# A transformer block with a split-precision MLP: two Strassen products after the chunk loop in place of the plain ones inside it

## The chip, the cores and the metric

One core of a Trainium2 chip runs the whole kernel. The metric is the device time of one launch in microseconds (us), the median of several runs. The engines are named as in the profile: PE is the matmul engine and PEld its weight loads, DVE the vector engine, ACT the scalar engine, POOL the GpSimd engine; SP issues all DMAs of this kernel.

## The reference

2048 tokens `x` of 1024 channels (`D`) pass one block. First an attention branch and a pooling branch, merged by gates, projected, added to `ALPHA * x` and layer-normalised. Then the part that the change touches, with `DFF` = 4096 hidden columns:

```python
def _mlp_sublayer(z, shift, scale, gate, w1, w2, g, b):
    u = _modulate(z, shift, scale)
    h = jnp.square(jax.nn.relu(u @ w1)) @ w2
    return _layernorm(ALPHA * z + gate * h, g, b)
```

Everything is fp32. The result before is a [2048, 1024] array.

## The kernel before, in words

PE multiplies fp32 numbers as products of two parts: `split` (L52) writes a high part (a rounding cast, by ACT) and a low part (the rest, by DVE, or by POOL where `lo_eng` says so), and each product is three matmuls, high by high, high by low and low by high (`mm3`, L59, and `chan_mm`, L680). Nearly all of the MLP's matmuls stream 512 columns against 128 by 128 stationary elements, and each has a weight load of its own.

Phase 1 (to about 865 us) makes `u`, q, k, v and the attention output and spills `u` and the output to DRAM (`u_scr`, `a_scr`). Phase 2 is a loop over two chunks `c` of 1024 tokens (L717). A chunk loads its `u` (`load_u`, L556: DMA into `raw`, then `split` into slots), does the pooling branch (`p_group`, `p_finish`, `pool_gate`), the attention gates, the branch products and the merge (`mg`), and the output projection (`out_mm`, L870). Per block `b` of 128 tokens follow `ln_affine` (the first layer norm, L891) and `ln1_u`, which normalises once more into `xn`; `u2_half` (L912) turns four blocks at a time on PE, modulates them on ACT and splits them. `accs[b]` holds the block's residual in SBUF through the MLP.

The MLP is the end of the chunk's body. For each group `fg` of 256 hidden columns, `mlp_in` (L945) multiplies `u2` with `w_mlp_in`, takes ReLU on ACT, squares on DVE and splits into `ht`; `mlp_out` (L959) multiplies `ht` with `w_mlp_out`, already scaled by the gate `gb[1]` on POOL, and DVE adds the product to `accs[b]`. After the last group `ln2` normalises and stores. The group after is always computed before the output product of this one, so that PE has work while ACT, DVE and POOL finish `ht`.

The slots are two sets, `a` (right side) and `b` (left side), 8 or 9 tiles for each of two tags, which change their parts between the chunks: `xs` takes `u`, `av`, then `accs`, `xn` and `ht`; `ys` takes the pooling tiles, `mg` and `u2`. Weights come through two `raw` tiles and two pairs `wh`, `wl`. A scheduler orders each engine's instructions by simulated time where the program doesn't fix it; a tile's slot comes free when the tile's last reader is done. All DMAs stand in one queue on SP, so a DMA that waits holds those behind it.

Numbers that the steps need: a chunk's MLP is 16 groups, each with 2 columns of 128, 2 halves of 512 tokens, 8 k tiles and 3 matmuls for the first product, and 8 blocks, 2 halves, 2 k tiles and 3 matmuls for the second: 16 * (96 + 96) = 3072 matmuls of 512 columns, 6144 for both chunks.

## Time and profile before

| what | value |
|---|---|
| runs | 3176.19 us median of 3 (3172.74 to 3176.82) |
| profiled execution, first to last instruction | 3174.3 us |
| PE busy | 3096.2 us, 98% of the span |
| DVE, ACT, POOL busy | 56%, 36%, 36% |
| chain that ended last | PE 87%, DVE 7% |
| DMA | 207.04 MB, mean 65 GB/s |

The profiled execution's own time is known as its span alone; the median is 1.9 us above it. The share of PE is a share of time in which any matmul is under way. Matmuls overlap, so one of 512 columns is shown as about 395 ns long though the next one starts earlier; the pace is read from how many start in a stretch.

### The profile page before, as it was taken

Reading aid. Unit: us, or ns where it says so; the run is one execution under the profiler, and the core shown is the slowest. Engines: PE = TensorE matmul, PEld = TensorE weight load, DVE = VectorE, ACT = ScalarE, POOL = GpSimd, SP = SyncE. Lnnn points to the kernel's source line nnn. Section 1 sums busy time; section 2 is a strip of 40 time slices with the busy share of each in tenths; the row PEclk is TensorE's granted clock in tenths of the full one; section 3 lists DMA queues with packets and bytes.
Section 4 is the critical chain, followed back from the end, with each engine's and each line's share of the span. In section 5 each row is a group of like instructions: output and inputs, shape, how many; then the busy total and the mean of one; then the engine's idle time right before and its main releaser. Section 6 shows DMA issues by size and latency. Waiting matters only on the chain.

```text
span 3174.3 us, 41663 instructions
## 1 busy us (share of the span) xinstructions
PE 3096.2 (98%) x16104; PEld 2616.7 (82%) x16104; DVE 1780.8 (56%) x3136; ACT 1128.2 (36%) x1985; POOL 1151.8 (36%) x1419
## 2 busy tenths in 40 slices
PE   8899999998999999899999999999999999999998
PEld 5799899997988889788888888788898788888886
DVE  5678788887774446644444455821448444444446
ACT  4577777777621222521112112311214311121111
POOL 2877777776420052422122221410234321222123
PEclk9999999999999999999999999999999999999999
DMA  7111111113154430211111112411321111111111
GB/s 244 35 30 41 35 31 41 35 31 105 28 160 128 146 107 28 67 41 53 53 41 54 40 53 66 142 52 40 107 93 54 40 53 44 50 53 41 53 40 53
DMA packets 157846, 207.04 MB, mean 65 GB/s; under 512 B 7248, under 2 KB 132304, under 8 KB 157648
## 3 DMA queue, kind: packets, MB, share of 16 engines
q1 hardware_dynamic: 157648, 204.38, 20.5%
q8 instruction: 127, 2.08, 0.3%
q14 instruction: 71, 0.58, 0.1%
HBM read 179.19 MB, written 25.17 MB: 64 GB/s over the span
## 4 chain that ended last, share of the span: by engine, by line
PE 87%; DVE 7%; DMA 2%; issue 2%; POOL 1%; ACT 1%; SPq 0%; DVEq 0%; POOLq 0%; ACTq 0%
PE ps_y L62 7%; PE ps_y L63 7%; PE ps_y L61 7%; PE ps_h L677 7%; PE ps_h L680 7%; PE ps_h L678 7%; PE ps_o L497 4%; PE ps_pt L480 4%; PE ps_s L444 3%; PE ps_ga L677 2%; PE ps_ga L680 2%; PE ps_ga L678 2%; PE ps_ab L677 2%; PE ps_ab L678 2%; PE ps_ab L680 2%; PE ps_s L445 2%
## 5 line engine op out<-in xcount | busy, mean ns | idle before, releaser
L57 POOL TENSOR_TENSOR ht<-r,ht 128x512 fp32r<-128x512 f32 x128 | 172.0, 1346 | 1009.0 <-ACT ht L54 946.3
L974 DVE TENSOR_TENSOR acc<-ps_y,acc 128x512 f32<-128x512 f32 x464 | 314.7, 689 | 366.6 <-PE ps_y L63 366.5
L54 ACT CAST wh<-raw 128x2048 fp32r<-128x2048 f32 (+1 forms) x102 | 189.1, 1857 | 828.9 <-PE ps_y L63 471.6
L678 PE MATMUL ps_h<-u,wh 128*128 128x512 f32 x1024 | 406.2, 397 | 10.3 <-DVE u L57 10.3
L62 PE MATMUL ps_y<-wl,ht 128*128 128x512 f32 x1024 | 405.0, 396 | 1.7 <-DVE wl L57 1.7
L680 PE MATMUL ps_h<-u,wl 128*128 128x512 f32 x1024 | 404.7, 396 | 0.0
L63 PE MATMUL ps_y<-wh,ht 128*128 128x512 f32 x1024 | 403.2, 394 | 0.0
L677 PE MATMUL ps_h<-u,wh 128*128 128x512 f32 x1024 | 401.3, 398 | 0.0
L61 PE MATMUL ps_y<-wh,ht 128*128 128x512 f32 x1024 | 400.6, 393 | 0.0
L57 DVE TENSOR_TENSOR wl<-raw,wh 128x2048 fp32r<-128x2048 f32 (+1 forms) x100 | 228.1, 2282 | 202.8 <-ACT wh L54 202.8
L951 DVE TENSOR_TENSOR r<-r 128x512 f32<-128x512 f32 x128 | 142.7, 1119 | 300.6 <-ACT r L950 300.6
L57 DVE TENSOR_TENSOR pl<-ps_pt,ph 128x512 fp32r<-128x512 f32 x312 | 212.6, 686 | 70.4 <-ACT ph L54 68.4
L678 PEld LDWEIGHTS ps_h<-u,wh 128*128 128x128 f32 x1024 | 193.2, 189 | 57.0 <-DVE u L57 12.1
L459 POOL TENSOR_SCALAR s<-s,sm 128x640 f32<-128x640 f32 (+1 forms) x256 | 202.3, 798 | 99.1 <-DVE sm L458 53.7
L456 ACT ACTIVATE s<-s,sm 128x641 f32<-128x641 f32 (+1 forms) x256 | 210.2, 822 | 66.6 <-DVE sm L450 66.1
L62 PEld LDWEIGHTS ps_y<-wl,ht 128*128 128x128 f32 x1024 | 192.1, 188 | 47.6 <-DVE wl L57 2.3
L61 PEld LDWEIGHTS ps_y<-wh,ht 128*128 128x128 f32 x1024 | 192.3, 188 | 46.9 <-ACT r L950 0.3
L680 PEld LDWEIGHTS ps_h<-u,wl 128*128 128x128 f32 x1024 | 193.5, 189 | 45.4
L677 PEld LDWEIGHTS ps_h<-u,wh 128*128 128x128 f32 x1024 | 193.2, 189 | 45.1
L450 DVE CUSTOM_DVE_ANT_0 s<-ps_s,mask,nsink 128x640 f32<-128x640 f32 (+1 forms) x256 | 211.4, 863 | 31.2 <-PE ps_s L445 30.6
L63 PEld LDWEIGHTS ps_y<-wh,ht 128*128 128x128 f32 x1024 | 192.2, 188 | 44.4
L54 ACT CAST ph<-ps_pt 128x512 fp32r<-128x512 f32 x312 | 179.7, 581 | 110.7 <-PE ps_pt L480 107.6
(217 smaller groups left out, 6931.2 us busy)
## 6 DMA issues: line engine op xcount, KB each, us to landing
raw<-w_mlp_in SPq DMA_DIRECT2D x32, 1024.0 KB, 5.5
raw<-w_mlp_out SPq DMA_DIRECT2D x32, 1024.0 KB, 4.8
raw<-w_in SPq DMA_DIRECT2D x19, 1024.0 KB, 5.5
raw<-w_ada SPq DMA_DIRECT2D x16, 1024.0 KB, 5.2
raw<-u_scr SPq DMA_DIRECT2D x8, 1032.0 KB, 5.4
adaw<-w_ada SPq DMA_DIRECT2D x16, 512.0 KB, 8.1
xt<-x SPq DMA_DIRECT2D x16, 512.0 KB, 3.6
u_scr<-u SPq DMA_DIRECT2D x32, 256.0 KB, 3.1
```

What stands on the lines that cost most here:

```text
L54: act.copy(hi, src)
L57: (lo_eng or dve).tensor_tensor(lo, src, hi.bitcast(F32), ALU.subtract)
L61: pe.matmul(ps, sh, mh, start=first, stop=False)
L62: pe.matmul(ps, sh, ml, start=False, stop=False)
L63: pe.matmul(ps, sl, mh, start=False, stop=last)
L450: dve.tensor_tensor_reduce(out=s[:, 0:n], in0=pieces[z][2], in1=mk[z], op0=ALU.add, op1=ALU.min, scale=-1.0 / math.sqrt(HD), scalar=nsink[ ...
L456: act.activation(s[:, 0:n + 1], s[:, 0:n + 1], AF.Exp, bias=sm[:, 0, j:j + 1], scale=-1.0, accum_out=sm[:, 1, j:j + 1])
L459: pool.tensor_scalar(s[:, 0:n], s[:, 0:n], sm[:, 2, j:j + 1], 1.0, ALU.mult, ALU.mult)
L677: pe.matmul(ps, wh[:, k, c:c + P], mh, start=k == 0, stop=False)
L678: pe.matmul(ps, wh[:, k, c:c + P], ml, start=False, stop=False)
L680: pe.matmul(ps, wl[:, k, c:c + P], mh, start=False, stop=k == KT - 1)
L974: dve.tensor_tensor(a, ps, a, ALU.add)
```

## The change

The MLP leaves the chunk loop. A chunk now ends with the first layer norm: its result goes to DRAM (`x1_scr`), and `u2_half` no longer splits but forms the seven left operands of a 2 by 2 block scheme (rows: alternating blocks of 128 tokens, columns: alternating k tiles) and stores them as planes of `us_scr`. The second `u2_half` of a chunk is put off: chunk 0's runs inside chunk 1's pooling branch, chunk 1's behind the loop.

After the loop, the first product runs over 32 pairs (`Pair`: chunk `c`, 256 hidden columns `n`). Each has seven products `p` (in `ORDER`) of 4 k tiles and 3 matmuls, into three PSUM tiles: X takes p = 1 then 2, Y takes 6, 7, 4, and Z takes 5, 3; between them DVE or ACT reads the running sum. Then come ReLU and square on ACT, sums of the hidden blocks on POOL, and seven stores of a plane each into `hs_scr`. Weight operands are summed on POOL and split by ACT and DVE, seven products ahead (`AHEAD`). The left operands of one chunk all stay in SBUF.

The second product takes one combination `p` over all 16 blocks of tokens (eight pairs `i`) before the next: 7 * 8 products of 16 hidden tiles and 3 matmuls. `h_fill` loads and splits the hidden planes two products ahead; `w2_fill` makes the weight operand of the next `p`, one of eight pieces after each product. `La` has 11 tiles, of which a combination needs 8; `w2` has four. The gate is applied to the finished sums (`resid`), and `ln2` follows with p = 4 and p = 3.

```diff
+    x1_scr = tc.dram_tile([T, D], F32, name="x1_scr")
+    g2_scr = tc.dram_tile([D], F32, name="g2_scr")
+    us_scr = [tc.dram_tile([P, 7, 4, 512], F32, name=f"us_scr{c}") for c in range(2)]
+    hs_scr = [[tc.dram_tile([P, 4, 16, P], F32, name=f"hs_scr{c}{p}") for p in range(7)] for c in range(2)]
+    t2_scr, t3_scr = (tc.dram_tile([P, 16, 512], F32, name=n) for n in ("t2_scr", "t3_scr"))
...
-    lp = ctx.enter_context(sbuf("ph2l"))
+    lpx = ExitStack()
...
+    late = []
     for c in range(2):
         t0 = c * CH
...
                 w = wcols(w_in, 1536 + gg * 256) if gg else w_first
+                if gg:
+                    run(late)
                 pooled = [p_finish(p_group(w, 2 * gg + i), 2 * gg + i) for i in range(2)]
...
+        def u2_half(h, c=c, t0=t0, xn=xn, ys=ys):
+            for kp in range(4):
+                f = slot(ys, 0, [P, 2, 512], F32, "u2f")
+                for kk in range(2):
+                    k = 2 * kp + kk
+                    ps = ps2("ps_u2", "u", 2)
+                    for i in range(4):
+                        pe.transpose(ps[:, i * P:(i + 1) * P], xn[4 * h + i][:, k * P:(k + 1) * P], ident)
+                    act.activation(f[:, kk], ps, AF.Identity, scale=mod[:, 32 + k, 0:1], bias=mod[:, 24 + k, 0:1])
+                v = f.rearrange("p k (b r t) -> p k b r t", r=2, t=P)
+                a11, a12, a21, a22 = v[:, 0, :, 0], v[:, 1, :, 0], v[:, 0, :, 1], v[:, 1, :, 1]
+                s = slot(ys, 1, [P, 4, 256], F32, "u2s")
+                sv = [s[:, i].rearrange("p (b t) -> p b t", t=P) for i in range(4)]
+                pool.tensor_tensor(sv[0], a21, a22, ALU.add)
+                pool.tensor_tensor(sv[1], sv[0], a11, ALU.subtract)
+                pool.tensor_tensor(sv[2], a11, a21, ALU.subtract)
+                pool.tensor_tensor(sv[3], a12, sv[1], ALU.subtract)
+                dst = us_scr[c][:, :, kp, h * 256:(h + 1) * 256]
+                for pl, t in enumerate((a11, a12, a22)):
+                    sp.dma_start(dst[:, pl].rearrange("p (b t) -> p b t", t=P), t)
+                sp.dma_start(dst[:, 3:7], s)
 
...
+            sp.dma_start(x1_scr[t0 + b * P:t0 + (b + 1) * P, :], accs[b])
             if b:
                 ln1_u(b - 1)
             if b == 5:
                 u2_half(0)
         ln1_u(7)
...
-        # ---- MLP ----
-        def mlp_w(fg):
-            return wcols(w_mlp_in, fg * 256, lo=pool if fg == 0 else None)
...
-        nf = DFF // 256
...
+        late = [lambda f=u2_half: f(1)]
...
+    run(late)
+    lpx.close()
+    ptx.close()
+    rpx.close()
+    ORDER = (1, 6, 2, 7, 5, 4, 3)
+    PLANE = {1: 0, 2: 1, 4: 2, 5: 3, 6: 4, 7: 5, 3: 6}
+    mp = ctx.enter_context(sbuf("mlp"))
+    m1 = ExitStack()
+    m1p = m1.enter_context(sbuf("mlp1"))
...
+    def rtile():
+        return mp.tile([P, 2, 4, P], F32R, name="R", tag="R", bufs=8)
+    def sttile(name):
+        return m1p.tile([P, 512], F32, name=name, tag="st", bufs=14)
+    w1v = w_mlp_in.rearrange("(k two p) n -> p two k n", two=2, p=P)
+    class Pair:
+        def __init__(self, c, n):
+            self.c, self.n, self.R = c, n, {}
+        def load(self):
+            self.raw = m1p.tile([P, 2, 4, 256], F32, name="sraw", tag="sraw", bufs=3)
+            for k in range(2):
+                sp.dma_start(self.raw[:, k], w1v[:, k, :, self.n * 256:(self.n + 1) * 256])
+            b11, b12, b21, b22 = self.b = [self.raw[:, k, :, h * P:(h + 1) * P] for k in range(2) for h in range(2)]
+            self.op = {1: b11, 2: b21, 3: b22, 4: b11, 7: b12}
+        def add(self):
+            b11, b12, b21, b22 = self.b
+            for p in (5, 6):
+                self.op[p] = m1p.tile([P, 4, P], F32, name="ext", tag="ext", bufs=4)
+            pool.tensor_tensor(self.op[5], b12, b11, ALU.subtract)
+            pool.tensor_tensor(self.op[6], b22, self.op[5], ALU.subtract)
+            pool.tensor_tensor(b12, b22, b12, ALU.subtract)
+        def step(self, p):
+            if p == 1:
+                self.add()
+            t = rtile()
+            split(t[:, 0], t[:, 1], self.op[p])
+            self.R[p] = t
+            if p == 1:
+                pool.tensor_tensor(self.b[0], self.b[2], self.op[6], ALU.subtract)
+        def square(self, t, src):
+            act.activation(t, src, AF.Relu)
+            act.activation(t, t, AF.Square)
+        def put(self, p, t):
+            sp.dma_start(hs_scr[self.c][PLANE[p]][:, :, self.n, :], t.rearrange("p (b t) -> p b t", t=P))
+        def prod(self, p, L):
+            if p in (1, 6, 5):
+                self.ps = ps2(f"ps_h{p}")
+                setattr(self, {1: "X", 6: "Y", 5: "Z"}[p], self.ps)
+            ps = self.X if p in (1, 2) else self.Z if p in (5, 3) else self.Y
+            r = self.R.pop(p)
+            for k in range(4):
+                m = L[k // 2]
+                mm = ((r[:, 0, k], m[:, 0, k % 2]), (r[:, 0, k], m[:, 1, k % 2]), (r[:, 1, k], m[:, 0, k % 2]))
+                for i, (a, b) in enumerate(mm):
+                    pe.matmul(ps, a, b, start=p in (1, 6, 5) and k == 0 and i == 0, stop=k == 3 and i == 2,
+                              skip_group_check=p not in (1, 6, 5))
+            add, sub = ALU.add, ALU.subtract
+            if p == 1:
+                self.x = sttile("cx")
+                act.copy(self.x, ps)
+            elif p == 6:
+                self.u2 = sttile("cu")
+                dve.tensor_tensor(self.u2, ps, self.x, add)
+            elif p == 2:
+                self.h11 = sttile("c11")
+                self.square(self.h11, ps)
+                self.put(1, self.h11)
+            elif p == 7:
+                self.u3 = sttile("cv")
+                dve.tensor_tensor(self.u3, ps, self.x, add)
+            elif p == 5:
+                h22 = self.u3
+                dve.tensor_tensor(h22, ps, self.u3, add)
+                self.square(h22, h22)
+                self.put(4, h22)
+            elif p == 4:
+                h21, h22 = self.x, self.u3
+                dve.tensor_tensor(h21, ps, self.x, add)
+                self.square(h21, h21)
+                self.s = s1, s2 = sttile("s1"), sttile("s2")
+                pool.tensor_tensor(s1, h21, h22, add)
+                pool.tensor_tensor(s2, s1, self.h11, sub)
+                pool.tensor_tensor(h21, self.h11, h21, sub)
+                self.put(5, s1)
+                self.put(6, s2)
+                self.put(7, h21)
+            else:
+                h12 = self.u2
+                dve.tensor_tensor(h12, ps, self.u2, add)
+                self.square(h12, h12)
+                self.put(2, h12)
+                s4 = sttile("s4")
+                pool.tensor_tensor(s4, h12, self.s[1], sub)
+                self.put(3, s4)
+    Lc = [{}, {}]
+    def l_fill(c, p):
+        raw = m1p.tile([P, 4, 512], F32, name="rw", tag="rw", bufs=2)
+        sp.dma_start(raw, us_scr[c][:, PLANE[p]])
+        Lc[c][p] = []
+        for j in range(2):
+            if (p, j) in ((1, 0), (1, 1), (6, 0)):
+                t = m1p.tile([P, 2, 2, 512], F32R, name="Lb", tag="Lb", bufs=3)
+            else:
+                t = mp.tile([P, 2, 2, 512], F32R, name="La", tag="La", bufs=11)
+            split(t[:, 0], t[:, 1], raw[:, 2 * j:2 * j + 2])
+            Lc[c][p].append(t)
+    pairs = [Pair(c, n) for c in range(2) for n in range(16)]
+    groups = [pairs[0:2]] + [[q] for q in pairs[2:14]] + [pairs[14:16], pairs[16:18]] + [[q] for q in pairs[18:]]
+    seq = [(g, p, q) for g in groups for p in ORDER for q in g]
+    for q in pairs[0:2]:
+        q.load()
+    prep = [(p, q) for _, p, q in seq]
+    AHEAD = 7
+    for i in range(AHEAD):
+        if i % 2 == 0:
+            l_fill(0, ORDER[i // 2])
+        prep[i][1].step(prep[i][0])
+    for p in ORDER[4:]:
+        l_fill(0, p)
+    for i, (g, p, q) in enumerate(seq):
+        n = q.c * 16 + q.n
+        if p == 1 and n + 2 < len(pairs):
+            pairs[n + 2].load()
+        q.prod(p, Lc[q.c][p])
+        if q is pairs[15]:
+            l_fill(1, p)
+        if i + AHEAD < len(prep):
+            prep[i + AHEAD][1].step(prep[i + AHEAD][0])
+    m1.close()
+    m2p = ctx.enter_context(sbuf("mlp2"))
+    w2v = w_mlp_out.rearrange("(n two p) d -> p two n d", two=2, p=P)
+    NI = 8
+    def w2_tile(src):
+        t = m2p.tile([P, 2, 512], F32, name="w2", tag="w2", bufs=4)
+        sp.dma_start(t, src)
+        return t
+    def w2_fill(p, j):
+        jj = slice(2 * j, 2 * j + 2)
+        b = lambda k, n: w2_tile(w2v[:, k, jj, n * 512:(n + 1) * 512])
+        if p == 1:
+            t = b(0, 0)
+        elif p == 6:
+            b12, t, b11 = b(0, 1), b(1, 1), b(0, 0)
+            pool.tensor_tensor(t, t, b12, ALU.subtract)
+            sp.dma_start(t3_scr[:, jj], t)
+            pool.tensor_tensor(b11, t, b11, ALU.add)
+            t = b11
+            sp.dma_start(t2_scr[:, jj], t)
+        elif p == 2:
+            t = b(1, 0)
+        elif p == 7:
+            t = w2_tile(t3_scr[:, jj])
+        elif p == 5:
+            t, b11 = b(0, 1), b(0, 0)
+            pool.tensor_tensor(t, t, b11, ALU.subtract)
+        elif p == 4:
+            t, t2 = b(1, 0), w2_tile(t2_scr[:, jj])
+            pool.tensor_tensor(t, t, t2, ALU.subtract)
+        else:
+            t = b(1, 1)
+        l = mp.tile([P, 2, 2, 512], F32R, name="La", tag="La", bufs=11)
+        split(l[:, 0], l[:, 1], t)
+        L2[p].append(l)
+    L2 = {p: [] for p in ORDER}
+    R2 = {}
+    def h_fill(p, i):
+        R2[p, i] = []
+        for z in range(2):
+            raw = m2p.tile([P, 8, P], F32, name="hraw", tag="hraw", bufs=3)
+            sp.dma_start(raw, hs_scr[i // 4][PLANE[p]][:, i % 4, 8 * z:8 * z + 8, :])
+            for k in (0, 4):
+                t = rtile()
+                split(t[:, 0], t[:, 1], raw[:, k:k + 4])
+                R2[p, i].append(t)
+    w2_fill(1, 0)
+    h_fill(1, 0)
+    for j in range(1, 8):
+        w2_fill(1, j)
+        if j == 4:
+            h_fill(1, 1)
...
+    st2 = m2p.tile([P, NB, 2, 6], F32, name="st2")
+    def ctile(name):
+        return m2p.tile([P, 512], F32, name=name, tag="C", bufs=24)
+    def resid(t, b, n):
+        cc = slice(n * 512, (n + 1) * 512)
+        xt = m2p.tile([P, 512], F32, name="x1", tag="x1", bufs=3)
+        sp.dma_start(xt, x1_scr[b * P:(b + 1) * P, cc])
+        pool.tensor_tensor(t, t, g2r[:, cc], ALU.mult)
+        dve.scalar_tensor_tensor(t, xt, ALPHA, t, op0=ALU.mult, op1=ALU.add)
+        dve.bn_stats(st2[:, b, n, :], t)
+    def ln2(halves, b, last):
+        mu, rs = ln_root(m2p, st2[:, b], "z")
+        nm = m2p.tile([P, 1], F32, name="nm", tag="nm", bufs=2)
+        dve.scalar_tensor_tensor(nm, mu, -1.0, rs, op0=ALU.mult, op1=ALU.mult)
+        for n, t in enumerate(halves):
+            cc = slice(n * 512, (n + 1) * 512)
+            if n == 0:
+                act.activation(t, t, AF.Identity, scale=rs, bias=nm)
+                pool.tensor_tensor(t, t, ln2gr[:, cc], ALU.mult)
+                pool.tensor_tensor(t, t, ln2br[:, cc], ALU.add)
+            else:
+                dve.scalar_tensor_tensor(t, t, mu, ln2gr[:, cc], op0=ALU.subtract, op1=ALU.mult)
+                dve.scalar_tensor_tensor(t, t, rs, ln2br[:, cc], op0=ALU.mult, op1=ALU.add)
+            sp.dma_start(out[b * P:(b + 1) * P, cc], t)
...
+    def prod2(p, i):
+        ps = ps2("ps_y")
+        for n in range(16):
+            r, m = R2[p, i][n // 4], L2[p][n // 2]
+            mm = ((r[:, 0, n % 4], m[:, 0, n % 2]), (r[:, 0, n % 4], m[:, 1, n % 2]), (r[:, 1, n % 4], m[:, 0, n % 2]))
+            for z, (a, b) in enumerate(mm):
+                pe.matmul(ps, a, b, start=n == 0 and z == 0, stop=n == 15 and z == 2)
+        del R2[p, i]
+        add = ALU.add
+        if p == 1:
+            cx[i] = ctile("cx")
+            act.copy(cx[i], ps)
+        elif p == 6:
+            cu[i] = ctile("cu")
+            dve.tensor_tensor(cu[i], ps, cx[i], add)
+        elif p == 2:
+            t = cx.pop(i)
+            dve.tensor_tensor(t, ps, t, add)
+            resid(t, 2 * i, 0)
+            sp.dma_start(x1_scr[2 * i * P:(2 * i + 1) * P, 0:512], t)
+        elif p == 7:
+            cv[i] = ctile("cv")
+            dve.tensor_tensor(cv[i], ps, cu[i], add)
+        elif p == 5:
+            c22[i] = ctile("c22")
+            dve.tensor_tensor(c22[i], ps, cv[i], add)
+            dve.tensor_tensor(cu[i], ps, cu[i], add)
+            resid(c22[i], 2 * i + 1, 1)
+        elif p == 4:
+            t = cv.pop(i)
+            dve.tensor_tensor(t, ps, t, add)
+            resid(t, 2 * i + 1, 0)
+            ln2((t, c22.pop(i)), 2 * i + 1, False)
+        else:
+            c11 = ctile("c11")
+            sp.dma_start(c11, x1_scr[2 * i * P:(2 * i + 1) * P, 0:512])
+            t = cu.pop(i)
+            dve.tensor_tensor(t, ps, t, add)
+            resid(t, 2 * i, 1)
+            ln2((c11, t), 2 * i, i == NI - 1)
+    todo = [(p, i) for p in ORDER for i in range(NI)]
+    for n, (p, i) in enumerate(todo):
+        prod2(p, i)
+        if p != 3:
+            w2_fill(ORDER[ORDER.index(p) + 1], i)
+        if n + 2 < len(todo):
+            h_fill(*todo[n + 2])
+    ms3.close()
```

## Rows read from the trace of the kernel before

**Rows 1.** The page: busy time of each engine, and the chain that ended last

```profile
PE 3096.2 (98%) x16104; PEld 2616.7 (82%) x16104; DVE 1780.8 (56%) x3136; ACT 1128.2 (36%) x1985; POOL 1151.8 (36%) x1419
...
PE 87%; DVE 7%; DMA 2%; issue 2%; POOL 1%; ACT 1%; SPq 0%; DVEq 0%; POOLq 0%; ACTq 0%
```

**Rows 2.** Windows of stages (header row names the columns)

```profile
core 0: us, PE busy (x) PEld busy (x) DVE busy (x) ACT busy (x) POOL busy (x), PEclk, DMA share, GB/s
1268.00:1302.00 34.00, 28.28 (x132) 22.22 (x131) 30.58 (x56) 19.88 (x35) 19.89 (x8) 0.95 0.30 92
1302.00:1332.00 30.00, 27.42 (x125) 22.17 (x125) 8.46 (x13) 16.66 (x27) 5.32 (x4) 0.94 0.01 2
1340.00:1990.00 650.00, 650.00 (x2803) 525.92 (x2802) 301.93 (x339) 129.21 (x149) 145.08 (x74) 1.00 0.17 53
2002.00:2024.00 22.00, 22.00 (x142) 22.00 (x141) 21.65 (x45) 7.78 (x16) 8.98 (x7) 1.00 0.27 90
2030.00:2110.00 80.00, 72.97 (x353) 62.89 (x352) 30.98 (x43) 22.94 (x31) 24.56 (x16) 0.96 0.25 84
2434.00:2490.00 56.00, 53.35 (x242) 42.77 (x242) 32.26 (x61) 32.28 (x56) 17.75 (x9) 0.95 0.14 43
2550.00:3100.00 550.00, 550.00 (x2368) 444.53 (x2367) 245.07 (x272) 105.70 (x122) 122.35 (x61) 1.00 0.15 46
```

**Rows 3.** PE's waits: one in time order (idle before), one summed by who ended it

```profile
2434.20 1.22 PE L678 MATMUL ps_h<-u,wh 128*128 128x512 f32 x2 [4.81 <-DVE u L57]
...
PE ps_pd L61 <- ACT poh L54: 7.0, 1, 7.0
```

**Rows 4.** Lines and tiles: durations in ns (min/median/max), first and last start

```profile
L63 PE MATMUL ps_out<-wh,mg x256: 276/281/363, 2335.2 to 2427.3; 128*128 128x256 f32 x128
L63 PE MATMUL ps_y<-wh,ht x1024: 388/394/405, 1334.9 to 3159.6; 128*128 128x512 f32 x171
L951 DVE TENSOR_TENSOR r<-r x128: 679/693/3984, 1302.8 to 3119.3; 128x512 f32<-128x512 f32 x128
L57 POOL TENSOR_TENSOR ht<-r,ht x128: 1264/1293/3221, 1304.2 to 3120.7; 128x512 fp32r<-128x512 f32 x128
L57 DVE TENSOR_TENSOR pl<-ps_pt,ph x312: 635/692/694, 99.5 to 862.8; 128x512 fp32r<-128x512 f32 x156
L57 POOL TENSOR_TENSOR wq<-wraw,wq x6: 2357/2398/2684, 46.0 to 62.7; 128x1024 fp32r<-128x1024 f32 x6
L54 ACT CAST ht<-r x128: 619/622/640, 1303.5 to 3120.0; 128x512 fp32r<-128x512 f32 x128
```

**Rows 5.** Groups by line and form: busy us, mean ns

```profile
L57 DVE TENSOR_TENSOR ul<-raw,uh 128x1032 fp32r<-128x1032 f32 x8 | 9.8, 1229 | 1.9 <-ACT uh L54 1.9
L54 ACT CAST uh<-raw 128x1032 fp32r<-128x1032 f32 x8 | 8.1, 1055 | 18.1 <-DMA raw<-u_scr 18.1
L918 ACT ACTIVATE u2f<-ps_u,mod 128x512 f32<-128x512 f32 x32 | 24.0, 773 | 24.0 <-PE ps_u L916 21.1 <-DVE u L57 2.7
L950 ACT ACTIVATE r<-ps_h 128x512 f32<-128x512 f32 x128 | 75.7, 597 | 263.6 <-PE ps_h L680 261.8 <-POOL ht L57 1.8
L951 DVE TENSOR_TENSOR r<-r 128x512 f32<-128x512 f32 x128 | 142.7, 1119 | 300.6 <-ACT r L950 300.6
L889 ACT ACTIVATE xn<-acc,nm,mv 128x1024 f32<-128x1024 f32 x16 | 19.9, 1244 | 9.7 <-DVE nm L888 9.7
```

**Rows 6.** A DVE and a POOL operation side by side, in order of time

```profile
2614.14 2.60 DVE L951 TENSOR_TENSOR r<-r 128x512 f32<-128x512 f32 x1 [4.91 <-ACT r L950]
...
2611.55 4.63 POOL L661 TENSOR_TENSOR raw<-raw,gb 128x2048 f32<-128x2048 f32 x1 [0.30 <-DMA raw<-w_mlp_out]
```

**Rows 7.** SP's queue in 400 to 700 us, then 2550 to 3100 us; landing times

```profile
q1 hardware_dynamic: 16224, 10.43, 12.9%
...
q1 hardware_dynamic: 14976, 25.17, 14.3%
...
raw<-w_mlp_in SPq DMA_DIRECT2D x32, 1024.0 KB, 5.5
wraw<-w_in SPq DMA_DIRECT2D x12, 512.0 KB, 3.9
```

**Rows 8.** Chain of waits, chunk 1's first layer norm; then the kernel's end

```profile
2453.86 1.29 POOL acc L900
2477.83 0.44 PE ps_u L916 x4
...
3166.09 0.21 DVE L982 BATCH_NORM_AGGREGATE mv<-st 128x2 f32<-128x12 f32 x1
...
3169.72 1.41 DVE L994 SCALAR_TENSOR_TENSOR acc<-acc,mv,lnp 128x512 f32<-128x512 f32 x2 [0.92 <-POOL mv L992]
```

More of the change, by code (lines that the diff above doesn't have):

```diff
@@ L100, in block_kernel @@
     psb = p1.enter_context(tc.tile_pool(name="psb", bufs=1, space=PSUM, reuse_waits="tile"))
-    rp = ctx.enter_context(sbuf("right", side="right"))
+    rpx = ExitStack()
+    rp = rpx.enter_context(sbuf("right", side="right"))
     wkx = ExitStack()
@@ L997, in ln2 @@
-        def ln2(b):
-            if c == 1 and b == 7:
-                return ln2_last(accs[b], slice(t0 + b * P, t0 + (b + 1) * P))
-            ln_affine(accs[b], ln2p)
-            sp.dma_start(out[t0 + b * P:t0 + (b + 1) * P, :], accs[b])
-        nf = DFF // 256
-        hts = [[[None, None] for _ in range(2)] for _ in range(nf)]
-        w = [mlp_w(0), mlp_w(1)]
-        mlp_in(w[0], hts[0], 0)
-        u2_half(1)
-        mlp_in(w[1], hts[1], 0)
-        mlp_in(w[0], hts[0], 1)
-        mlp_in(w[1], hts[1], 1)
@@ L1011, in block_kernel @@
-        ln2p = ln_params(ln2_g, ln2_b)
-        for fg in range(nf):
-            if 0 < fg < nf - 1:
-                wn = mlp_w(fg + 1)
-                for h in range(2):
-                    mlp_in(wn, hts[fg + 1], h)
-            if c == 1 and fg == nf - 2:
-                continue
-            parts = [(hts[f], mlp_w2(f)) for f in ((fg - 1, fg) if c == 1 and fg == nf - 1 else (fg,))]
-            for b in range(8):
-                mlp_out(parts, b, fg == 0)
-                if fg == nf - 1:
-                    ln2(b)
+        late = [lambda f=u2_half: f(1)]
@@ new lines, in block_kernel @@
+    rows = []
+    for name, v in (("g2", g2_scr), ("ln2g", ln2_g), ("ln2b", ln2_b)):
+        r = m2p.tile([P, D], F32, name=name)
+        sp.dma_start(r, v.partition_broadcast(P))
+        rows.append(r)
+    g2r, ln2gr, ln2br = rows
+    st2 = m2p.tile([P, NB, 2, 6], F32, name="st2")
[8 more added lines that the diff above has]
+        dve.bn_stats(st2[:, b, n, :], t)
```

65 lines of the change are left out of this document (7 added, 58 removed).

## The prediction, on record before the changed kernel ran

> **What bounds the kernel.** The page comes first: PE is busy for 98% of the span and makes 87% of the chain that ended last, the other engines are under 60% [rows 1]. A share says nothing of single stages, so the windows come next. In the middle of both MLPs PE is never idle, at a granted clock of 1.00, and starts 2803 instructions in 650 us and 2368 in 550 us: 0.232 us for each, and all are matmuls of 512 columns [rows 2]. So a matmul left out there is worth 0.232 us, as long as DVE (46%), ACT and POOL (under 25%) keep up. At the MLP's seams PE does wait. Chunk 0's first two stretches hold 5.7 and 2.6 us without a matmul, at clocks of 0.95 and 0.94; chunk 1's holds 2.7 us at 0.95 [rows 2], and just ahead of it lies a wait of 4.8 us for DVE [rows 3]. Chunk 1's pooling stage has one wait of 7.0 us [rows 2, 3].
>
> **The sum, against the profiled execution's span of 3174.3 us; the median of the runs is 1.9 us above that.**
>
> 1. Matmuls. Before: 2 * 3072 = 6144. After: first product 32 pairs * 7 products * 4 k tiles * 3 = 2688; second 56 products * 16 * 3 = 2688; together 5376. Each keeps its 512 columns and its own weight load, so I keep the pace: 768 fewer at 0.232 us is **-178 us**.
>
> 2. Seams that go. The idle time above is 5.7 + 2.6 + 2.7 + 4.8 = 15.8 us; the clock's shortfall is 5% of 34, 6% of 30 and 5% of 56 us, 6.3 us. Both MLP starts vanish: **-22 us**. `u2_half`'s turning on PE stays. Of the pooling stage's 7.0 us wait and its clock's 3.2 us (4% of 80) I take half, since `ln2` leaves POOL and DVE there but `u2_half`'s sums come: **-5** (0 to -10).
>
> 3. Between the chunks. Before, chunk 1's `u` was loaded and split beneath chunk 0's last MLP groups. Now the pooling product follows the output projection directly. The slots of `ul` are those of `mg`'s second halves, read until the last `out_mm`. Then eight low parts of 1.23 us on DVE [rows 5], 9.8 us, stand in one queue with the layer norm of the last two blocks; in the 34 us behind that point DVE was busy for 30.6 already [rows 2], of which only `u2`'s low parts leave. The first pooling group is 72 matmuls of 344 columns at 22/142 = 0.155 us [rows 2], 11.2 us; I put DVE's part at 22. Loss about 11, and 1 of clock: **+12**. Ends: 0 (the low parts are early) and 25 (the whole layer norm ahead of them). The 16 stores of `x1_scr` stand in SP's queue behind POOL's last scaling of each block; what is queued behind them is `raw` of the next weights, with two tiles loaded ahead.
>
> 4. Start of the first product. Before, MLP matmuls of the chunk's first half covered the layer norm of block 7. Now chunk 1's second `u2_half` stands ahead of them on PE. Its chain from the last `out_mm`: two DVE operations of 256 columns, 0.7 us at half the 0.69 of 512 [rows 4], the root and its neighbours 3 us (3.6 at the kernel's end, from 3166.1 to 3169.7 [rows 8]), an ACT half 0.8, two POOL scalings of 1.29 us [rows 8], two statistics at 0.7 as for other DVE operations of 512 columns, the root 3, the normalisation 1.24, then eight modulations of 0.77 us [rows 5]: 13 + 6 = 19 us. The loads of the first pairs and planes (5.5 us for 1 MB [rows 7]) wait for the closed pools' slots, partly beneath this. A group of two pairs is then 24 matmuls, 5.6 us, for each p; DVE owes it two left parts at 1.23, two weight parts and up to two sums at 0.69 [rows 4, 5], 5.2 us: it just holds. With 3 us of half clock and 6 us until the first operands are split: **+28**. Ends: 10 (matmuls wait for a load alone) and 50 (as before, where block 7's turning came at 2478, 50 us after the projection's end at 2427.6 [rows 4, 8]).
>
> 5. Pace of the first product. A pair is 84 matmuls, 19.5 us. ACT: seven casts at 0.62, a copy and four ReLUs and four squares at 0.6 [rows 4, 5], 9.7 us. DVE: seven low parts and five sums at 0.69, 8.3 us. POOL: eight sums at 1.29, 10.3 us. All are below 19.5. But DVE with two SBUF inputs and POOL exclude each other: a squaring that takes 0.69 us took 2.60 and ended 0.56 us after POOL's scaling, begun earlier, had ended [rows 6]. With an input in PSUM there was no such wait (0.694 us at most in 312 [rows 4]). So 10.3 + 4.8 = 15.1 us of a pair's 19.5 are exclusive. Between p's on the same PSUM tile DVE or ACT has one product, 2.8 us, to read it. I take 0.3 us lost per pair: **+10** (0 to 40). DMA: seven stores of 512 packets at 12.9% * 16 * 300 / 16224 = 38 ns, and 1 MB at 25.17 MB / (14.3% of 550 us) = 320 GB/s [rows 7]: 11.8 of 19.5 us. Nine issues a pair fit on SP.
>
> 6. Second product. A product is 48 matmuls, 11.1 us; its four weight casts and low parts, one left piece (1.06 us ACT, 1.23 DVE) and its sums fit. Its entry is covered: w2 pieces take `La` tiles as the last pair frees them. The critical spot is the change of p: three spare `La` tiles take three pieces early, and five wait for the old combination's last product, 22 us before the last is needed. For p = 6 a piece is three loads, two POOL sums of 2.4 us [rows 4] and two stores, with four `w2` tiles: about 3.9 [rows 7] + 2.4 + 2.4 + (1.06 + 1.23 [rows 5]) = 11 us in series, so one or two pieces come late. p = 5 and 4 need two loads and one sum, about 8.6 us. I take 8 us for p = 6, 2 each for the two others and 3 for the entry: **+15**. Ends: 0 and 60 (p = 6 in strict series, 20; two others 15 each; entry 10).
>
> 7. End. Before, 14.5 us lie behind the last matmul [rows 4]. The new chain has a POOL gate product more (1.29) and ends in two POOL scalings in place of two DVE ones, but without the separate store order; nothing either way (-3 to 3). The fewer weight scalings on POOL were hidden.
>
> Sum: -178 - 22 - 5 + 12 + 28 + 10 + 15 = -140, so 3034.3, and 3036 as a median.
>
> **Rivals.**
>
> A. PSUM hand-over paces the first product. Of 224 products 128 (p = 2, 7, 4, 3) go on in a bank that an engine has just read. If DVE stands in a low part that POOL holds up (2.60 us [rows 6]) and then needs 0.69, PE waits about 0.5 us: 128 * 0.5 = 64 us instead of 10, 3090. For it: DVE's queue is in order. Against it: POOL is busy for about half of a pair, and most of its sums are 1.29, not 4.63 us.
>
> B. The second product waits for DMA and pieces. While p = 1 runs, 8 MB of hidden planes and 20 MB for p = 6 move, 29.4 million bytes in 89 us; at the MLP's 320 GB/s that is 92 us, at the attention's 10.43 MB / (12.9% of 300 us) = 269 GB/s it is 109 [rows 7]. With 20 us there, and 15 at each of the two other changes of p and 10 at the entry, the time is 3036 + 45 = 3081. The Trainium skill's DMA: Bandwidth & Descriptors, section Bandwidth, speaks for this: it wants at least 1 MiB in a DMA for three quarters of the peak, and these are halves of that. No row here shows pieces of that size in a dense stream.
>
> C. The covers hold: of the added costs only about 20 us of the first product's start are left. 3176 - 205 + 20 = 2991. For it: the scheduler may lift matmuls or loads over the turning. Against it: PE's order is fixed by hand there.
>
> D. Slower than before: POOL and DVE pace the first product. Their exclusive 15.1 us are 15 operations. The gain of 140 us and the 10 already counted are gone when a pair takes 19.5 + 150/32 = 24.2 us, so when each of the 15 costs 0.6 us more than alone. At 0.8 a pair is 27.1 us and the time 3036 + 32 * 7.6 - 10 = 3269. For it: mean durations of 1.12 beside a median of 0.69 for the squaring, and single ones up to 3.98 [rows 4, 5]. Against it: those waits were mostly for the long scalings that are gone. The Trainium skill's GPSIMD Engine Reference, section Key points, says that GpSimd shares its SBUF interfaces with VectorE and contends with two-input instructions; the trace agrees by that 2.60 us.
>
> **How the numbers follow.** The forecast has 0.60, A 0.15, B 0.13, C 0.08, D 0.04. The predicted time is the forecast's. Its own range, with one or two terms at an end, is 3005 to 3065; A and B take the upper bound to 3100, C's upper half the lower one to 3000. Left out are D, most of C and mishaps of A and B beyond 3100, under 2 in 10. A measurement of this kernel can tell 0.2%, 6 us, from no change. All cases but D, and a sum of A, B and all upper ends, are faster by more: 0.95; within 0.2%: 0.01; slower: 0.04.
>
> **What would show it.** The page's PE matmuls fall by 768. Windows within a group of single pairs show 84 matmuls in 19.5 to 20 us at a clock of 1.00; under A or D PE's longest waits there name DVE or ACT, or POOL. Between the projection's end in chunk 1 and the first product lie about 28 us. Waits inside the second product name `w2` pieces of p = 6 above all; under B they name DMAs of hidden planes too. The prediction is wrong if the pace of matmuls in clean stretches is not 0.232 us, or if the waits in the two products together pass 90 us.

## The result, and the profile after

The changed kernel takes 3037.52 us (median of four runs, 3034.49 to 3039.96) against 3175.6 us before (four runs, 3172.74 to 3176.82): a ratio of 0.9567, 95% interval 0.9554 to 0.9581, 138 us less. The prediction was 3036. The profiled execution's span is 3038.2 us, 136.1 below the 3174.3 of before. The number was met; several of its terms were not, and they cancel. The views show where.

The page of the kernel after, to be read against [rows 1]: busy time, then the chain that ended last.

```profile
PE 2909.0 (96%) x15336; PEld 2481.3 (82%) x15336; DVE 1819.1 (60%) x3201; ACT 1369.1 (45%) x2462; POOL 1380.6 (45%) x1638
...
PE 35%; DVE 2%; DMA 2%; POOL 2%; issue 1%; ACT 1%; SPq 0%; POOLq 0%; ACTq 0%
```

PE has 768 instructions fewer, as counted ahead. Its share fell by two points: the kernel has more time in which nothing multiplies. Windows of the stages say which (same columns as [rows 2]): the seam between the chunks, the pooling stage, the way to the first product, that product (three rows), the seam to the second, and that product (three rows).

```profile
1274.00:1310.00 36.00, 25.64 (x139) 23.01 (x139) 31.23 (x57) 21.37 (x33) 23.11 (x22) 0.81 0.91 277
1310.00:1400.00 90.00, 90.00 (x461) 78.40 (x460) 30.12 (x27) 28.17 (x39) 30.76 (x26) 1.00 0.37 114
1711.30:1762.80 51.50, 13.19 (x58) 8.67 (x56) 22.68 (x48) 21.72 (x36) 38.47 (x44) 0.59 0.78 259
1762.80:1800.00 37.20, 33.73 (x129) 26.82 (x130) 34.53 (x33) 24.17 (x35) 12.85 (x9) 0.88 0.71 233
1800.00:2050.00 250.00, 250.00 (x1105) 207.01 (x1104) 137.65 (x163) 132.74 (x218) 159.92 (x110) 1.00 0.55 164
2050.00:2380.00 330.00, 329.73 (x1455) 272.73 (x1454) 184.83 (x214) 172.15 (x283) 194.80 (x129) 1.00 0.52 158
2380.00:2393.00 13.00, 0.91 (x5) 0.41 (x3) 1.92 (x2) 3.19 (x6) 4.98 (x4) 0.61 0.73 233
2393.00:2510.00 117.00, 103.75 (x427) 82.85 (x427) 62.03 (x58) 44.71 (x65) 39.59 (x16) 0.94 0.90 324
2510.00:2600.00 90.00, 89.53 (x383) 73.51 (x384) 40.27 (x52) 30.58 (x43) 0.00 (x0) 0.97 0.54 175
2600.00:2690.00 90.00, 90.00 (x399) 74.53 (x398) 47.95 (x62) 26.75 (x40) 19.52 (x10) 1.00 0.57 183
```

Two things stand out. Where PE is never idle and the clock is 1.00, 1105 matmuls start in 250 us and 399 in 90, against 2803 in 650 before [rows 2]. Their starts lie 226 or 227 ns apart, 226.7 in the mean; before, the same form of matmul came every 232.2 ns, with single distances from 224 to 241. And behind the projection the losses stand at the entries of the two products, 1711 to 1800 and 2380 to 2510, with 0.3 us of idle time in between. PE's waits from the projection's end in chunk 1 to the end, then three at the seam between the chunks, 1250 to 1420 (us in total, times, longest):

```profile
PE ps_h L1039 <- ACT Lb L59: 21.9, 1, 21.9
PE ps_y L1220 <- ACT R L59: 12.1, 1, 12.1
PE ps_y L1220 <- ACT La L59: 11.3, 3, 5.4
PE ps_u L929 <- ACT xn L900: 11.2, 3, 5.0
PE ps_u L929 <- ACT u2f L930: 5.2, 5, 2.1
PE ps_h L1039 <- DVE Lb L62: 3.5, 2, 3.0
PE ps_y L1220 <- DVE La L62: 2.3, 4, 0.8
PE ps_h L1039 <- ACT cx L1044: 0.3, 1, 0.3
...
PE ps_p L686 <- DVE ul L62: 4.7, 1, 4.7
PE ps_u L929 <- ACT u2f L930: 4.1, 5, 1.9
PE ps_p L685 <- ACT uh L59: 1.5, 2, 1.0
```

Of the PSUM hand-over of rival A, a wait for `cx`, `cu` or `cv`, there is one of 0.3 us, and no wait names POOL.

### The profile page after: what moved, and what is told of

It reads as the page before. It is cut to its first block, busy times and chain, and to the rows that moved or that the text cites. A ratio compares the mean times of both kernels' runs of the same rounds, so it can differ in the third digit from the quotient of the medians.

```text
span 3038.2 us, 42601 instructions
## 1 busy us (share of the span) xinstructions
PE 2909.0 (96%) x15336; PEld 2481.3 (82%) x15336; DVE 1819.1 (60%) x3201; ACT 1369.1 (45%) x2462; POOL 1380.6 (45%) x1638
## 5 line engine op out<-in xcount | busy, mean ns | idle before, releaser
L1220 PE MATMUL ps_y<-La,R 128*128 128x512 f32 x2688 | 619.4, 393 | 25.8 <-ACT R L59 12.1
L1220 PEld LDWEIGHTS ps_y<-La,R 128*128 128x128 f32 x2688 | 508.9, 190 | 136.4 <-ACT La L59 13.7
L1039 PE MATMUL ps_h<-La,R 128*128 128x512 f32 x2112 | 485.2, 390 | 0.3 <-ACT cx L1044 0.3
L1039 PEld LDWEIGHTS ps_h<-La,R 128*128 128x128 f32 x2112 | 397.2, 188 | 83.3 <-ACT cx L1044 0.7
L62 DVE TENSOR_TENSOR R<-hraw,R 128x512 fp32r<-128x512 f32 x224 | 198.0, 890 | 150.7 <-ACT R L59 150.2
L486 PE MATMUL ps_pt<-ident,s 128*128 128x128 f32 x1248 | 189.7, 274 | 12.4 <-DVE pl L62 8.2
L62 DVE TENSOR_TENSOR R<-sraw,R 128x512 fp32r<-128x512 f32 x160 | 146.3, 917 | 77.3 <-ACT R L59 76.8
L486 PEld LDWEIGHTS ps_pt<-ident,s 128*128 128x128 f32 x1248 | 151.6, 141 | 43.1 <-DVE pl L62 11.3
L1039 PE MATMUL ps_h<-Lb,R 128*128 128x512 f32 x576 | 139.5, 396 | 25.4 <-ACT Lb L59 21.9
L66 PE MATMUL ps_out<-wh,mg 128*128 128x256 f32 x512 | 143.1, 281 | 0.0
L67 PE MATMUL ps_out<-wl,mg 128*128 128x256 f32 x512 | 142.8, 280 | 0.0
```

What stands on the lines that cost most here:

```text
L62: (lo_eng or dve).tensor_tensor(lo, src, hi.bitcast(F32), ALU.subtract)
L66: pe.matmul(ps, sh, mh, start=first, stop=False)
L67: pe.matmul(ps, sh, ml, start=False, stop=False)
L486: pe.transpose(pt[:, c:c + P], self.s.probs[2 * z + j][:, o:o + P], ident)
L1039: pe.matmul(ps, a, b, start=p in (1, 6, 5) and k == 0 and i == 0, stop=k == 3 and i == 2, skip_group_check=p not in (1, 6, 5))
L1220: pe.matmul(ps, a, b, start=n == 0 and z == 0, stop=n == 15 and z == 2)
```

## Experiments

Most of the variants below have one run each. The four runs of the changed kernel spread over 5.5 us, so for a single run a difference of a few us is read from the waits and spacings of its trace, not from its time.

**Why a 512-column matmul became 5.5 ns shorter.** Two answers were set against each other: the shape of the products, or the place of their operands. R tiles of the changed kernel lie 4096 B apart, `La` tiles 8192 B; before, the slots were 4128 or 4160 B apart. So each was padded in turn.

```diff
-        return mp.tile([P, 2, 4, P], F32R, name="R", tag="R", bufs=8)
+        return mp.tile([P, 2 * 4 * P + 8], F32R, name="R", tag="R", bufs=8)[:, 0:8 * P].rearrange("p (z k n) -> p z k n", z=2, n=P)
```

> The changed kernel starts a matmul every 0.2267 us in both MLP products, while 512-column matmuls of the kernel before, and of the gates in both kernels, come every 0.232 to 0.233. This kernel gives each weight tile R 32 bytes more, so that the tiles lie 4128 bytes apart, as the slots of the kernel before do, in place of 4096. Theory 'place of the operands': the pace goes back to about 0.232, so 5376 * 0.0053 = 28 us more, some 3066 us. Rival 'shape of the products' (matmuls per PSUM tile, order of the combinations): 0.2267 and 3038 us as without the edit.

The other padding is the same 8 elements behind each `La` and `Lb` (`[P, 2048 + 8]`):

> The same with the streamed operands: the tiles La and Lb get 32 bytes more each (8224 bytes apart in place of 8192), R as it was. Theory 'place of the operands', if what counts is how weights and stream lie to each other: the pace goes to about 0.232, some 3066 us. If only the weight tiles' place counts: 0.2267, 3038 us. Rival 'shape of the products': 0.2267, 3038 us.

Measured: 3065.64 and 3064.03 us, with mean spacings of 232.3 and 232.5 ns. In each, the sequence of distances repeats as the tiles come round (every 96 matmuls, eight R tiles, in the first; every 84, the 14 left tiles of a pair, in the first product of the second). The shape is the same, so the place of the operands makes the difference. A pad of 128 B (`2 * 4 * P + 32`) was to say which places:

> After the first two padded kernels: how far must a weight tile be from the streamed tile's place? R tiles 4224 bytes apart (128 bytes more each), so that the eight tiles, used in turn, stand 0, 128, 256, 384, 512, 640, 768 and 896 bytes off the place of La, counted in multiples of 512. Theory 'multiples of 512 bytes are free' (inside a tile the k tiles are 512 bytes apart and cost nothing): every fourth product, in tiles 0 and 4, keeps 0.2267 us per matmul, the other six take 0.229 to 0.234, so 0.230 to 0.231 on the whole and 18 to 24 us more: 3056 to 3062 us. Rival 'equal place within 2048 or 4096 bytes only': at most one of eight products keeps 0.2267; 3060 to 3066 us.

Measured: 3062.23 us and 231.4 ns. The time is the one that the rival gave, but neither form of the theory fits the distances. Eight tiles stand at eight different places, yet the sequence repeats every 24 matmuls, two tiles, and once in these 24 it holds still near 227 (distances of successive starts in ns, from the trace):

```
R 4224 B apart: 236 224 231 236 228 232 231 227 227 226 227 232 241 233 231 231 229 230 232 241 232 231 232 233
kernel after:   227 227 226 227 227 226 227 227 226 227 227 226 227 227 226 227 227 226 227 227 226 227 227 226
```

Two shifts without padding: 64 B ahead of all tiles of the stage (`mp.tile([P, 16], F32, name="fill")` as its pool's first), and 1024 B between R and `La` alone (`[P, 256]`, ahead of the first `La`).

> In e5_pad_r128 no weight tile kept 0.2267 us, tiles 0, 2, 4, 6 took 0.2303 and the others 0.2324; there La also lay 1024 bytes further on. Here 64 unused bytes lie ahead of both R and La, so all operands of both products move by 64 bytes together and keep their pitches and their distances. Theory 'distance': only how weights and stream lie to each other counts, the pace stays 0.2267, 3038 us. Rival 'own place': each operand's own address counts, the pace goes to 0.229 to 0.234, 3050 to 3066 us.

> 1024 unused bytes lie between R and La: R stays where it was with its pitch of 4096, all La tiles move by 1024 bytes with their pitch of 8192. Theory 'distance or place of the stream': the pace goes to about 0.230, the value of tile 0 in e5_pad_r128, 3055 us. Rival 'pitch of the weight tiles': 0.2267 stays, 3038 us.

Measured: 3036.82 and 3037.01 us, both with 226.7 ns. So a shift of all operands together doesn't matter, and neither does a distance of 1024 B. The pitches of 4096 and 8192 B as such still fitted all this, but so did something else: in all three kernels with the short spacing, R and `La` leave the same remainder when their address is divided by 256 B. A shift of `La` by 128 B with every pitch kept tells these apart:

```diff
         Lc[c][p] = []
+        if (c, p) == (0, 6):
+            mp.tile([P, 32], F32, name="fill")
```

> The weight tiles R keep their places and their pitch of 4096 B; La and Lb move up by 128 B, so that R and La stand 128 B apart by the remainder of their addresses to 256 B (0 in the kernel after, in the kernel with both shifted by 64 B and in the one with La shifted by 1024 B). In the padded kernel with a pitch of 4224 B the 512-column products repeat every 24, two R tiles, though its eight tiles stand at eight places: so only the remainder to 256 B seems to count, and in the tile whose remainder equals that of La the spacing settles at 226 to 227 ns after some seven products, while it never does in the other. Theory (equal remainders to 256 B of the two operands give the short spacing): now no tile has it, 0.231 to 0.233 us in both products, 5376 x 0.0045 to 0.0065 = 24 to 35 us, so 3061 to 3072 us. Rival (what counts is that successive R tiles keep one remainder, whatever La's; or the pitch of 4096 B): 0.2267 us as after, 3035 to 3040 us.

Measured: 3064.6 us (four runs, 3062.78 to 3067.15), ratio to before 0.9655, interval 0.9639 to 0.9671. Its windows, beside the rows of 1800 to 2050 and 2600 to 2690 above (of the engines PE alone, then clock, DMA share and GB/s):

```profile
1800.00:2050.00 250.00, 250.00 (x1073) 1.00 0.54 154
2600.00:2690.00 90.00, 90.00 (x387) 1.00 0.57 179
```

Here 1073 matmuls start in the 250 us that held 1105; distances alternate between 229 or 230 and 237 or 238 ns, 233.3 in the mean. One unused tile of 128 B costs 27 us. The seven kernels together (remainders to 256 B of the addresses at which the program places the tiles; the first and the last time are medians of four runs, the others of one run each):

| kernel | R | `La` | spacing, ns | us |
|---|---|---|---|---|
| after | 64 | 64 | 226.7 | 3037.5 |
| both shifted by 64 | 128 | 128 | 226.7 | 3036.8 |
| `La` shifted by 1024 | 64 | 64 | 226.7 | 3037.0 |
| R 4224 apart | 64, 192 | 64 | 231.4 | 3062.2 |
| R 4128 apart | eight | 64 | 232.3 | 3065.6 |
| `La` 8224 apart | 64 | eight | 232.5 | 3064.0 |
| `La` shifted by 128 | 64 | 192 | 233.3 | 3064.6 |

Equal remainders give the short spacing in both products; the same pitches without them don't. The chip that a variant ran on isn't the reason for the pads: four unpadded variants that follow below, two on the chip of the pads of 32 B (loads from ACT, stores from ACT) and two on that of the pad of 128 B (late rows, load order), keep 226.7 ns. That 256 B is the step, and not a larger one, rests on the 24 matmuls of the pitch of 4224 B alone. What in the chip does this is not shown. That the 232.2 ns of before have this cause is likely, since the remainders of its slots differ, but no run aligned them there, so it isn't shown.

**Why the first product starts 51.5 us after the projection.** The end of the chain ahead of it (start, us, what):

```profile
1747.46 1.28 SPq L1001
...
1750.46 11.04 DMA rw<-us_scr
...
1761.68 1.05 ACT Lb L59
...
1762.75 1.27 DVE Lb L62
```

The last plane was stored, four weight loads (L1001) passed SP, and then the first left operand was read, which took 11.0 us; the turning had ended by 1741, POOL's sums by 1746. The operand that is read first is not what was stored last: the first pairs are those of chunk 0, and `l_fill(0, ...)` reads planes of chunk 0, whose last store went out long before. ACT's last normalisation and last modulations of chunk 1 come late, too:

```profile
1392.46 0.36 SPq L942 DMA_DIRECT2D us_scr<-u2s  x1
...
1732.31 1.24 ACT L900 ACTIVATE xn<-acc,nm,mv 128x1024 f32<-128x1024 f32 x1 [0.92 <-DVE nm L899]
...
1740.07 1.64 ACT L930 ACTIVATE u2f<-ps_u,mod 128x512 f32<-128x512 f32 x2 [0.35 <-PE ps_u L929]
```

So the first product doesn't wait for the data of the last stores. Are the loads held up by their place in SP's queue, or by the slots? In the first run the first two pairs' weights and the first two left operands are loaded from ACT's queue (`q.load(act)`, `l_fill(0, ORDER[i // 2], act if i < 4 else sp)`):

> The loads of the first two pairs' weights and of the first two left planes are issued by ACT instead of SP. Theory 'SP's order': these loads stood in SP's queue behind the last stores of the second half of chunk 1 (the last at 1746 us), so now they land beneath the turning on PE and the first product starts 10 to 18 us earlier, 51 us after the projection's end become 33 to 41. Rival 'slots': the loads wait for tiles of the closed pools, and the start moves by under 3 us.

Measured: 3041.02 us; the first matmul comes 57 us after the projection's end, later than the 51.5, which neither theory said. ACT's first load of the weights stood until 1740.85, when a store from a slot had landed, and the second left operand's until 1753.9, when the last store, which took 11.3 us beside the loads, had landed. The chain names these stores, by line and in order of time:

```profile
by line: DMA us_scr<-u2s 16.2%; issue 7.6%; DVE R L62 7.0%; DMA us_scr<-u2f 6.4%; PE ps_u L929 6.1%; POOL acc L909 6.0%; POOL acc L911 5.3%; POOL u2s L935 5.0%; POOL u2s L936 4.6%; POOL u2s L937 4.0%; POOL u2s L938 2.7%; DVE st L88 2.7%; AC
...
1736.31 4.51 DMA us_scr<-u2f
...
1742.56 11.32 DMA us_scr<-u2s
```

So the queue alone was not the hold: behind it stand the slots, which come free when the stores out of them have landed. The next run keeps SP and changes only the order: the left operand of the first product ahead of the second pair's weights.

> Only the order of the first loads: pair 0, the plane of p = 1, pair 1, then the others, instead of both pairs first. Theory 'the loads themselves stand on the path at the start of the first product': 1 MB less lies ahead of the first matmul, 3 to 4 us at 260 GB/s, so it starts 47 to 48 us after the projection's end instead of 51.5; part of it may come back as a wait for pair 1. Rival 'slots': the plane's tile is free only later, and nothing moves.

Measured: 3039.20 us. The first matmul comes 48.4 us after the projection, 3 earlier, but PE's next wait is 6.38 us instead of 2.97: the second pair is late in its turn. Nothing is left of it. What remains is a chain of layer norm, turning, sums, stores, loads and split of which only single links were moved.

**Why the second product is slow to enter.** SP's queue at the change (start, us):

```profile
2385.41 0.51 SPq L1027 DMA_DIRECT2D hs_scr<-s  x1
2386.02 0.59 SPq L1126 DMA_DIRECT2D w<-w_mlp_out  x1
```

and PE's timeline there (in brackets the idle time before):

```profile
2393.03 3.76 PE L1220 MATMUL ps_y<-La,R 128*128 128x512 f32 x7 [12.12 <-ACT R L59]
...
2405.97 0.50 PE L1220 MATMUL ps_y<-La,R 128*128 128x512 f32 x1 [4.41 <-ACT La L59]
...
2509.80 0.79 PE L1220 MATMUL ps_y<-La,R 128*128 128x512 f32 x1 [5.37 <-ACT La L59]
```

The first weight load of the second product stands right behind the last store of the hidden planes, which waits for the last sums: PE had ended at 2380.9, five us before. The last pair's stores were put into ACT's queue (L1027):

```diff
-            sp.dma_start(hs_scr[self.c][PLANE[p]]...
+            (act if self is pairs[-1] else sp).dma_start(hs_scr[self.c][PLANE[p]]...
```

> The seven stores of the very last pair of the first product are issued by ACT instead of SP. Theory 'SP's order': the second product's loads stood behind them (the first went out at 2386.0 us, 0.1 us after the last store's issue), so the loads go out up to 15 us earlier and the 12.1 us without a matmul between the products, and most of the 7.7 us of waits just behind, shrink by 10 to 18 us together. Rival 'slots': the loads wait for the first product's tiles, and the gap stays within 3 us.

Measured: 3033.40 us. The rows of the three waits:

```profile
2383.73 3.84 PE L1220 MATMUL ps_y<-La,R 128*128 128x512 f32 x7 [6.74 <-ACT R L59]
...
2399.95 0.80 PE L1220 MATMUL ps_y<-La,R 128*128 128x512 f32 x1 [6.90 <-ACT La L59]
...
2503.31 0.79 PE L1220 MATMUL ps_y<-La,R 128*128 128x512 f32 x1 [5.14 <-ACT La L59]
```

The gap falls by 5.4 us, and 2.5 of them come back in the wait for the weight pieces; gap and waits together shrink by 3.3 us, where 10 to 18 were forecast. SP's order was part of the hold and no more. The pieces compete for the DMA with three broadcast rows that nothing needs before p = 2 (L1180), so the next run, on top of this edit, loads the rows one by one during p = 6:

```diff
         prod2(p, i)
+        if p == 6 and i in (2, 4, 6):
+            sp.dma_start(rows[i // 2 - 1], row_src[i // 2 - 1][1].partition_broadcast(P))
```

> The last pair's stores from ACT as in e3_act_puts, and the three rows for the gate and the second layer norm (0.5 MB each, broadcast) are loaded during p = 6 instead of ahead of the second product. Theory 'DMA rate': the entry of the second product waits for bytes (324 GB/s at a DMA share of 0.90 in its first 117 us), so 1.57 million bytes fewer are worth 5 us of the waits there, 16.5 us in e3_act_puts become 11 to 12, and the time is about 3029 us. Rival 'pieces': each piece's own load, cast and low part pace it; the waits stay within 2 us, 3033 us.

Measured: 3029.86 us; the wait of 6.90 is 4.25, the one at p = 6 is 4.37 instead of 5.14. The rows were part of it, about half of what was forecast.

**Whether POOL and DVE could have paced the first product (rival D).** Five of the eight sums that POOL makes for each pair are made twice, with the same result:

```diff
             pool.tensor_tensor(self.op[5], b12, b11, ALU.subtract)
+            pool.tensor_tensor(self.op[5], b12, b11, ALU.subtract)
```

> Five of a pair's eight POOL sums are done twice in the first product (same result), 13 operations of 1.24 us instead of 8. A pair's 84 matmuls take 19.0 us. Theory 'DVE's two-input operations and POOL exclude each other': 13 * 1.24 + 7 * 0.69 = 20.9 us a pair, so POOL and DVE become the bound and the first product takes 50 to 70 us more. Rival 'they run side by side, or only a started operation is waited for': POOL's 16.1 us stay below 19.0 and the time stays within 8 us of 3038.

Measured: 3103.29 us, 66 more. The window 1850 to 2050, then PE's longest wait of the stage, and two of DVE's groups in the window (busy time, mean ns): a low part with both inputs in SBUF, and a sum with one in PSUM.

```profile
1850.00:2050.00 200.00, 188.08 (x818) 152.51 (x817) 111.85 (x118) 94.94 (x157) 193.04 (x132) 1.00 0.50 148
...
PE ps_h L1041 <- ACT cx L1046: 39.8, 25, 7.1
...
L62 DVE TENSOR_TENSOR R<-sraw,R 128x512 fp32r<-128x512 f32 x49 | 57.7, 1177 | 43.1 <-ACT R L59 43.0
...
L1064 DVE TENSOR_TENSOR cx<-ps_h,cx 128x512 f32<-128x512 f32 x10 | 6.9, 692 | 5.3 <-PE ps_h L1041 5.3
```

A pair is 84 * 200 / 818 = 20.5 us, forecast 20.9; POOL is busy for 193 of 200 us, and DVE's low parts of R take 1.18 us in the mean, against 0.69 alone [rows 4], while its sums with an input in PSUM stay at 0.69 beside the same POOL. So the exclusion of D is real. That GpSimd contends with VectorE's instructions with two SBUF inputs is what the Trainium skill's GPSIMD Engine Reference says in its Key points, and these rows agree. In the changed kernel DVE pays it too, but on nothing that PE waits for:

```profile
L62 DVE TENSOR_TENSOR R<-sraw,R 128x512 fp32r<-128x512 f32 x51 | 44.6, 875 | 20.9 <-ACT R L59 20.8
```

**The edits together**: stores from ACT, late rows, the load order, and three of the four sums of the last `u2_half` on DVE (`e = dve if c == 1 and h == 1 else pool`), in five runs.

> The edits of e6_rows_late and e7_load_order together, and for the last half chunk three of the four sums of u2_half on DVE instead of POOL. From 3037.5: e6_rows_late took 8 us off; the load order alone moved the first matmul by 3 us and gave it back. Theory 'tiles of the closed pools': the first loads wait for the stores of these sums, POOL does 16 of them in a row in 11 us (1735.0 to 1746.0); with 12 on DVE they end 3 to 4 us earlier, and the first product starts 45 us after the projection's end instead of 51.5; the time is about 3026 us (3022 to 3031). If the sums are not on the path: 3030 us.

Measured: 3032.03 us (3030.13 to 3034.54), ratio to before 0.9551, interval 0.9538 to 0.9564. It beats both kernels, the changed one by 5.5 us with intervals that overlap. The forecast of 3022 to 3031 is missed. PE's waits at the two entries are 19.2 (21.9) and 6.8 us (12.1), and 5.9 is the one behind the first products (3.0). The sums' place saves nothing: the first matmul comes 48.2 us after the projection, as with the load order alone. The edit hardly moved the sums, as the last store of a plane still goes out 34.0 us after the projection's end (34.7 in the changed kernel), so it doesn't tell whether they are on the path. In the profiled execution the projection itself ended 3.4 us earlier than in that of the changed kernel, and no edit lies ahead of it, so part of the gain is not the edits'.

## Why the prediction was right, step by step

| step | predicted | measured in the profiled execution |
|---|---|---|
| 1. matmuls | -178 | -178, and 5376 * 5.5 ns = -30 by the spacing |
| 2. MLP seams; pooling | -22; -5 | -22; -10 |
| 3. between the chunks | +12 | 10.4 idle + 19% of 25.6 busy: +15 |
| 4. start of the first product | +28 | +52 |
| 5. pace of the first product | +10 | 0.3 |
| 6. second product | +15 | +35 |
| 7. end | 0 | -2 |
| sum | -140 | -140; spans -136 |

**Step 1** failed where it says "I keep the pace". The count was exact, but 0.232 us is no property of a matmul of 512 columns: the pads and the shift of 128 B bring it back and beyond with the same matmuls, so before it most likely belonged to the places of the operands. The prediction named this as what would make it wrong, and by that sentence it was. The shift by 128 B shows what the change gives without this gift: 3064.6, a gain of 110 instead of 138 us. Its spacing of 233.3 lies 1.1 ns above that of before, so at the pace of before the gain would be some 6 us larger (an estimate, 5376 * 1.1 ns).

**Step 2.** The pooling stage has no wait left (90.00 of 90 us, clock 1.00), so all 10.2 us of its loss went, the end of the range.

**Step 3** was near in size: 10.4 us of idle time stand where 11 were put. A wait of 4.7 us for `ul`'s low parts is there as described; 4.1 more are for the modulations of `u2_half`, which the step left out, and the clock of 0.81 costs 5 us instead of 1.

**Step 4** was mis-sized in two terms. The layer norm and the modulations, put at 13 + 6 = 19 us, took 22 + 8: the last `xn` ended at 1733.6 and the last modulation at 1741.7, with the projection's end at 1711.4. The prediction counted POOL's scalings of the layer norm alone; in the same queue stand the sums of the other half chunk. In the run with loads from ACT, where `xn` is as late, the chain of 70 us runs through both, 11.3% for the scalings (L909, L911) and 16.3% for the sums (L935 to L938), 11 us. No run took these sums away. The other term is the loads, taken as "partly beneath this", with the row of 5.5 us for a load of 1 MB [rows 7]. They lie behind it, 21 us where 9 were put: sums to 1746, issues to 1750.5, 11.0 us for a load behind 2 MB of others, 2.3 us of split. The reason given, the closed pools' slots, showed when the loads left SP's queue; in that queue they stood behind the last stores. Of the 51.5 us, 13.2 are turning at a clock of 0.59 (7.8 at 1.00), so 43.7 are lost, and 3.5 idle and 12% of 37 us of clock behind it: 52. The upper end given was 50.

**Step 5** fell to nothing: PE is idle for 0.3 us between 1800 and 2380. Rivals A and D are excluded by that. The exclusion that D builds on is real, but its condition was absent: the margin of 19.0 (84 * 0.2267) to 15.1 us held, and the doubled sums show that it was not large.

**Step 6** failed at "Its entry is covered" (3 us). The entry is 12.1 us idle, 7.7 in five short waits and the clock of 0.94 over 117 us (7): 27. The cover ended where the last pair's sums began, and one queue took the stores ahead of the loads. At p = 6 the wait is 5.4 + 0.5, where 8 was put; the other changes of p have none. The rest is clock, 3% of 90 us. For **rival B** this is its condition in part, but DMA moved faster than it was priced: 324 GB/s as a mean at a share of 0.90 from 2393 to 2510, 360 GB/s when busy, in pieces of 512 KB. The Trainium skill's DMA: Bandwidth & Descriptors, section Bandwidth, asks for at least 1 MiB in a DMA for three quarters of the peak. Here halves of that moved no less when busy than the 320 GB/s of the loads of 1 MB before.

**Rival C**, that the covers hold, was right for step 5 and wrong for 4 and 6.

So the forecast's centre was met by luck: about 45 us too much cost in one half (spacing, pooling, step 5) stood against 47 too little in the other (steps 3, 4 and 6). It is a fair result for the range, and no proof of the steps. The steps as measured give 4 us more than the spans do; where these lie stays open.

## What to carry to other kernels

Before a matmul's spacing is carried to a new layout, read whether it jitters: a steady one and a jittering one of the same form differed by 5 to 7 ns here, on 5376 matmuls. Give the two operands of a matmul stream tiles whose addresses have the same remainder to 256 B, by the tiles' pitch and what is allocated ahead of them. Where one stage takes over the queue and the SBUF of another, the seam costs the whole series of last sum, store, issue, landing and split, however well the stages are covered inside, and even where the data that the new stage reads first has long been stored.
